# Gated linear attention in a hybrid mixer layer: level scores and state reads by 64 by 64 quarters of the matmul array

## The chip, the cores and the metric

One core of a Trainium2 chip runs the whole layer. The metric is the time of one execution on the device, in microseconds (us), and it is better when it is lower.

## What is computed

The reference is one layer over 2048 latent tokens and 256 context tokens of 1024 features. Two mixers run in parallel in both directions over the tokens: a gated linear attention (GLA, 4 heads, 64 key features, 128 value features, with a decay for each key feature), and a gated delta rule (GDN, 4 heads). Their outputs are normalised, gated and merged. The change touches GLA alone. In chunks of tokens it computes

```
diff = bi[:, :, :, None, :] - bi[:, :, None, :, :]
dec = exp(where(causal[:, :, None], diff, -inf))
att = einsum('bhtd,bhsd,bhtsd->bhts', qi, ki, dec)
o = einsum('bhtd,bhde->bhte', qi * exp(bi), s) + einsum('bhts,bhse->bhte', att, vi)
s_new = s * exp(bl)[..., None] + einsum('bhsd,bhse->bhde', ki * exp(bl - bi), vi)
```

where `bi` is the running sum of the log decay, `s` the state, and `t`, `s` are query and key tokens. The forward and the backward direction are added.

## The kernel before

The kernel has three stages. The first (up to some 1386 us) projects the input with matmuls, runs the short convolution and solves the triangular systems of GDN. The second, `phase_mix`, scans over the 16 latent chunks of 128 tokens, forward from the first and backward from the last at the same time. The third (from some 1796 us) multiplies by the output weights. Only the scan is touched.

For one chunk GLA needs the scores of 128 keys by 128 queries for 4 heads, where the decay depends on key, query and feature. It builds them by levels: at level m (64, 32, 16, 8, 4, 2) the keys of one block of m tokens meet the queries of the neighbouring block, both scaled by decays that are counted from the border between the two, so that one matmul over 64 features gives the scores of all such pairs. Forward and backward scores share a matrix, as one lies above the diagonal and the other below. The pairs of neighbours (m = 1) and the diagonal come from products of single features (`gla_ones`, `gla_near`, and `diag` from the first stage).

The parts of a step, in the order in which `gla_step` (L1263) gives them out; every `yield` is a place where `weave` (L1412) may let another generator go on, in proportion to the weights given in `phase_mix` (24 for `gla_step`, 12 for each direction of `gdn_scan`), and the framework then places the instructions on each engine's queue by its own planning:

- `gla_split` and L1268: the log decays as two fp32r parts (ACT and POOL); the diagonal into the score tile `at` (POOL).
- `gla_ends` (L1120): sums of decays by matmuls with a constant (L1117), exponentials on ACT (L1126, L1128), keys times decays on POOL (L1129).
- For the previous step: `gla_near` (L1234) finishes its scores, `gla_state` (L1306) makes the new states (L1313, L1323).
- `gla_group` (L1191), three times, for levels 64 and 32, then 16 and 8, then 4 and 2: sums (L1117), exponentials (L1205, L1208), queries times decays on DVE (L1214) and keys times decays on POOL (L1215).
- For the previous step: `gla_out` (L1327) multiplies scores by values (L1332) and scaled queries by the state (L1337) into two PSUM banks, one for the even and one for the odd heads; its `done` copies them out (ACT L1345 in the first eight steps, DVE L1347 with the earlier output added in the other eight).
- `gla_lev` (L1243), three times, one for each group: the level matmuls (L1250) into a slot of the PSUM tile `lv`, then the copies from the slot into `at`: level 64 by two copies on ACT (L1258), the others by a predicated copy on DVE with a mask from `am` (L1261). The first call is placed behind gla_out of the previous step, the second after the third group, the third at the end of the step.

The tile `lv` has two slots of 128 queries; `slot` takes them in turn. Each level matmul uses 64 rows of the array (the features of one head) and all 128 columns, so that the two heads of a pair can run at once. In the first eight steps the outputs of a chunk are written to memory; in the other eight the chunk's other direction is read back, added and normalised (`finish`, L1383: squares on ACT L1392 to L1394, scaling on POOL L1395, transposes L1399, DVE L1400).

Of the kernel before, what the change touches and what calls it, by code (L numbers as in the profile page):

```python
# [11 lines left out]
F32 = mybir.dt.float32  # L12
# [3 lines left out]
I32 = mybir.dt.int32  # L16
AF = mybir.ActivationFunctionType
ALU = mybir.AluOpType
AX = mybir.AxisListType
PSUM = bass.MemoryType.PSUM  # L20
DRAM = bass.MemoryType.DRAM

P = 128
# [7 lines left out]
NCTX = CTX // P  # L31
# [7 lines left out]
LEVELS = (64, 32, 16, 8, 4, 2, 1)  # L39
# [45 lines left out]
def const_i32():  # L85
    s = np.arange(P)[:, None]
    out = np.zeros((P, 2, len(MASK_LEVELS), 64), np.int32)
    for d in range(2):
        for i, m in enumerate(MASK_LEVELS):
            t = later_cols(d, m)[None, :]  # L90
            out[:, d, i, :] = ((s // (2 * m)) == (t // (2 * m))) & ((s // m) != (t // m))
    t = s.T
    pairs = [((s // (2 * m)) == (t // (2 * m))) & ((s // m) != (t // m)) for m in LEVELS[1:]]
    return np.concatenate([out.reshape(P, -1), *[x.astype(np.int32) for x in pairs]], 1)


class Build:
# [1045 lines left out]
    def slot(self):  # L1143
        self.nslot += 1
        return self.lv[:, :, self.nslot % 2]

# [44 lines left out]
    def gla_group(self, r, i0):  # L1191
        nc, q, k, at = self.nc, r["q"], r["k"], r["at"]
        E = self.gE.tile([P, 2, 2, 2, P], F32, name="E", bufs=3)
        ql = self.gq.tile([P, 2, 2, P], F32, name="ql", bufs=3)
        cols = (2 * P + i0 * P, 4 * P + i0 * P)
        for ct in range(2):
            ps = self.pe()
# [3 lines left out]
            for li in range(2):  # L1201
                m = LEVELS[i0 + li]
                s = ps[:, 256 * li:256 * li + 256]
# [12 lines left out]
        yield  # L1216
        return [(at, [E[:, ct, li, 1] for ct in range(2)], ql[:, li], LEVELS[i0 + li]) for li in range(2)]

# [15 lines left out]
    def gla_near(self, r):  # L1234
        nc, at, w = self.nc, r["at"], r["near"]
        pd = self.pe()
        for ct in range(2):
            nc.tensor.matmul(pd[:, 2 * ct:2 * ct + 2], w[:, ct], self.bones, start=True, stop=True)
        B = [P, 4, P]
        nc.vector.copy_predicated(at, self.am[:, len(LEVELS) - 2].unsqueeze(1).broadcast_to(B),  # L1240
                                  pd[:, 0:4].unsqueeze(2).broadcast_to(B))

    def gla_lev(self, levs, behind=None):  # L1243
        nc, got = self.nc, []
        for at, ks, ql, m in levs:
            ps = self.slot()
            for ct in range(2):
                for hp in range(2):
                    rows = slice(64 * hp, 64 * hp + 64)
                    mm = nc.tensor.matmul(ps[:, hp, ct], ks[ct][rows], ql[rows, ct], start=True, stop=True)  # L1250
                    self.behind(mm, behind)
                    self.last_lev = mm
            got.append((self.byhalf(at), ps, m))
        for at, ps, m in got:
            if m == 64:
                for x in range(2):
                    rows, cols = slice(64 * x, 64 * x + 64), slice(64 - 64 * x, 128 - 64 * x)
                    nc.scalar.copy(at[rows, :, :, cols], ps[rows, :, :, cols])  # L1258
            else:
                i = LEVELS.index(m) - 1  # L1260
                nc.vector.copy_predicated(at, self.am[:, i].unsqueeze(1).unsqueeze(1).broadcast_to([P, 2, 2, P]), ps)  # L1261

    def gla_step(self, f, b, prev):  # L1263
        nc = self.nc
        self.gla_split(f)
        self.gla_split(b)
        at = f["at"] = f["kp"].tile([P, 4, P], F32, name="at", bufs=1)
        nc.gpsimd.tensor_tensor(at, self.diag[:, f["c"] - NCTX, :].unsqueeze(2).broadcast_to([P, 4, P]),  # L1268
                                self.ident.unsqueeze(1).broadcast_to([P, 4, P]), op=ALU.mult)
        yield  # L1270
        self.gla_ends(f)
        yield
        if prev is not None:
            self.gla_near(prev[0])
            S = self.gla_state(prev)
            yield
        levs = yield from self.gla_group(f, 0)
# [6 lines left out]
        if prev is not None:  # L1284
            out, done = self.gla_out(prev, S)
        self.gla_lev(levs, out if prev is not None else None)
        if prev is not None:
# [4 lines left out]
        last = yield from self.gla_group(f, 4)  # L1292
        yield
        self.gla_lev(more)
        yield
# [31 lines left out]
    def gla_out(self, pair, S):  # L1327
        nc = self.nc
# [5 lines left out]
        for d, r in enumerate(pair):  # L1334
            for h in range(4):
                ct, rows = h // 2, slice(64 * (h % 2), 64 * (h % 2) + 64)
                mm = nc.tensor.matmul(po[h % 2][:, d, ct], r["qe"][rows, ct], S[d][rows, ct], start=False,  # L1337
                                      stop=d == 1 and h >= 2, skip_group_check=True)

# [82 lines left out]
    def phase_mix(self):  # L1422
# [14 lines left out]
        for x in range(2):  # L1437
            nc.vector.memset(self.bones[64 * x:64 * x + 64, x:x + 1], 1.0)
            nc.vector.memset(self.bones[64 * x:64 * x + 64, 1 - x:2 - x], 0.0)
        self.am = mp.tile([P, len(LEVELS) - 1, P], I32, name="am")  # L1440
        wt = mp.tile([P, 2, WL], F32R, name="wt")
# [3 lines left out]
        self.ppe = self.pool("ppe", 3, PSUM, ctx=ctx)  # L1445
        self.lv = self.pool("ppg", 1, PSUM, ctx=gctx).tile([P, 2, 2, 2, P], F32, name="lv")
        self.nslot, self.last_lev = 0, None
# [246 lines left out]
```

## Time and profile before

| | us |
|---|---|
| median of 3 runs | 2175.05 |
| lowest and highest | 2174.11 to 2176.63 |
| the profiled execution | 2176.2 |
| its span, first to last instruction | 2174.4 |
| TensorE marked busy | 2089.3 (96%) |
| DVE, ACT, POOL busy | 1237.0, 888.1, 867.7 |

The profile is one execution of its own. A busy TensorE is not one at its peak, because matmuls are pipelined and the marked time of each runs to its end; how close their starts stand tells more. The chain of work that ended last is followed back from the last instruction, at each step to what released it or to the instruction before it on its engine. An fp32 matmul stands in the records as two matmuls, each with its weight load (PEld). A row of windows gives the busy time, with the number of instructions, in the order TensorE (PE), its weight loads (PEld), DVE, ACT, POOL, those that were asked for.

### The profile page before, as it was taken

Reading aid. Unit: us, or ns where it says so; the run is one execution under the profiler, and the core shown is the slowest. Engines: PE = TensorE matmul, PEld = TensorE weight load, DVE = VectorE, ACT = ScalarE, POOL = GpSimd, SP = SyncE. Lnnn points to the kernel's source line nnn. Section 1 sums busy time; section 2 is a strip of 40 time slices with the busy share of each in tenths; the row PEclk is TensorE's granted clock in tenths of the full one; section 3 lists DMA queues with packets and bytes.
Section 4 is the critical chain, followed back from the end, with each engine's and each line's share of the span. In section 5 each row is a group of like instructions: output and inputs, shape, how many; then the busy total and the mean of one; then the engine's idle time right before and its main releaser. Section 6 shows DMA issues by size and latency. Waiting matters only on the chain.

```text
span 2174.4 us, 39781 instructions
## 1 busy us (share of the span) xinstructions
PE 2089.3 (96%) x15072; PEld 1753.6 (81%) x15072; DVE 1237.0 (57%) x2183; ACT 888.1 (41%) x2180; POOL 867.7 (40%) x779
## 2 busy tenths in 40 slices
PE   5999999999999999999999999899989988999998
PEld 2688888888888888777777777788888887999888
DVE  3813555556777554555555555566678876344333
ACT  3644255554552223343444443344455554112111
POOL 2410122222231015665666662556566655222331
PEclk9999999999999999999999999999999989999999
DMA  7323122222222224344444443878779958443322
GB/s 279 110 85 115 50 68 64 67 62 66 61 65 81 74 84 138 118 146 146 141 147 151 129 139 114 300 279 307 262 262 312 299 177 265 131 127 116 102 85 81
DMA packets 275004, 315.67 MB, mean 145 GB/s; under 512 B 22280, under 2 KB 206716, under 8 KB 274812
## 3 DMA queue, kind: packets, MB, share of 16 engines
q1 hardware_dynamic: 274812, 313.12, 44.5%
q8 instruction: 119, 1.95, 0.4%
q14 instruction: 73, 0.60, 0.1%
HBM read 203.20 MB, written 109.84 MB: 144 GB/s over the span
## 4 chain that ended last, share of the span: by engine, by line
PE 83%; DVE 5%; ACT 4%; DMA 4%; issue 2%; SPq 1%; POOL 1%; DVEq 0%; POOLq 0%; ACTq 0%
PE pz L370 46%; PE pz L1647 8%; PE pm L1578 7%; PE pe L1117 2%; PE pz L1079 1%; PE pe L935 1%; PE pl L987 1%; PE pl L994 1%; PE lv L1250 1%; PE pl L995 1%; DMA g<-dg 1%; PE pz L1058 1%; DVE ql L1214 1%; PE pq L613 1%; ACT E L1208 1%
## 5 line engine op out<-in xcount | busy, mean ns | idle before, releaser
L370 PE MATMUL pz<-hi,wh 128*128 128x512 f32 (+1 forms) x1560 | 621.7, 399 | 1.6 <-DVE hi L133 1.6
L370 PE MATMUL pz<-lo,wh 128*128 128x512 f32 (+1 forms) x1560 | 600.6, 385 | 1.8 <-POOL lo L134 1.8
L370 PE MATMUL pz<-hi,wl 128*128 128x512 f32 (+1 forms) x1520 | 588.6, 387 | 0.0
L370 PEld LDWEIGHTS pz<-lo,wh 128*128 128x128 f32 x1560 | 294.8, 189 | 51.3 <-POOL lo L134 3.7
L370 PEld LDWEIGHTS pz<-hi,wh 128*128 128x128 f32 x1560 | 294.4, 189 | 48.0 <-DVE hi L133 2.5
L370 PEld LDWEIGHTS pz<-hi,wl 128*128 128x128 f32 x1520 | 286.3, 188 | 53.8 <-issue 0.4
L134 POOL TENSOR_TENSOR wl<-w,wh 128x1024 fp32r<-128x1024 f32 x44 | 108.8, 2475 | 437.3 <-ACT wh L131 311.9
L568 DVE SCALAR_TENSOR_TENSOR acc<-zpad,cw,acc 128x1024 f32<-128x1024 f32 x192 | 271.4, 1414 | 6.7
L1578 PE MATMUL pm<-yh,wab 128*128 128x256 f32 x1024 | 190.5, 287 | 0.9 <-ACT wab L131 0.9
L872 DVE CAST_PREDICATED U<-kit,pl 128x256 f16<-128x256 int32 x216 | 91.2, 431 | 139.4 <-PE pl L995 135.6
L1578 PEld LDWEIGHTS pm<-yh,wab 128*128 128x128 f32 x1024 | 163.5, 195 | 1.8 <-ACT wab L131 1.0
L1647 PE MATMUL pz<-wo,mh 128*128 128x512 f32 (+1 forms) x528 | 160.6, 387 | 0.0
L1578 PE MATMUL pm<-yl,wab 128*128 128x256 f32 x512 | 146.9, 287 | 0.2 <-POOL yl L134 0.2
L988 ACT CAST ppb<-pl 128x256 f16<-128x256 f32 x216 | 73.6, 374 | 167.6 <-PE pl L987 161.2
L1215 POOL TENSOR_TENSOR E<-E,ak 128x256 f32<-128x256 f32 x96 | 80.9, 863 | 101.8 <-ACT E L1205 51.6
L1647 PEld LDWEIGHTS pz<-wo,mh 128*128 128x128 f32 x528 | 98.2, 189 | 20.0
L134 DVE TENSOR_TENSOR sql<-sq,sqh 128x512 fp32r<-128x512 f32 (+1 forms) x36 | 28.0, 804 | 142.0 <-ACT sqh L131 141.8
L623 POOL TENSOR_TENSOR acc<-acc,sq 128x512 f32<-128x512 f32 x32 | 51.1, 1605 | 138.4 <-ACT sq L622 90.6
L1647 PE MATMUL pz<-wo,ml 128*128 128x512 f32 (+1 forms) x264 | 101.5, 385 | 0.0
L1578 PEld LDWEIGHTS pm<-yl,wab 128*128 128x128 f32 x512 | 100.2, 196 | 0.7 <-POOL yl L134 0.4
L134 POOL TENSOR_TENSOR yl<-wr,yh 128x1024 fp32r<-128x1024 f32 x16 | 40.2, 2529 | 135.7 <-ACT yh L131 135.7
L1652 DVE TENSOR_TENSOR mt<-pz,gtb 128x512 f32<-128x512 f32 (+1 forms) x33 | 22.3, 675 | 117.0 <-PE pz L1647 114.8
(297 smaller groups left out, 4182.9 us busy)
## 6 DMA issues: line engine op xcount, KB each, us to landing
dgate<-ob SPq DMA_DIRECT2D x96, 256.0 KB
gd<-dgd SPq DMA_DIRECT2D x32, 768.0 KB
w<-in_w_in SPq DMA_DIRECT2D x44, 512.0 KB
qk<-dqkv SPq DMA_DIRECT2D x32, 512.0 KB
ga<-dgate SPq DMA_DIRECT2D x64, 256.0 KB
dqkv<-acc SPq DMA_DIRECT2D x192, 64.0 KB
dgd<-tm SPq DMA_DIRECT2D x36, 256.0 KB
dgd<-n SPq DMA_DIRECT2D x36, 256.0 KB
```

What stands on the lines that cost most here:

```text
L134: getattr(nc, lo).tensor_tensor(dst_lo, src, dst_hi.bitcast(F32), op=ALU.subtract)
L370: nc.tensor.matmul(ps[:, 0:n], a[:, kk, :], b[:, kk, :], start=(k == 0), stop=(k == last - 1))
L568: nc.vector.scalar_tensor_tensor(acc, src, wcol, acc, op0=ALU.mult, op1=ALU.add)
L613: nc.tensor.matmul(u[4][:, 0:u[2]], self.ones, u[3][i], start=(i == 0), stop=(i == 1))
L623: nc.gpsimd.tensor_tensor(v, v, r, op=ALU.mult)
L872: self.nc.vector.copy_predicated(out, mv, data)
L988: nc.scalar.copy(ppl, pc.rearrange("p h (j i) -> p h j i", i=m))
L1117: self.nc.tensor.matmul(out, g[:, i, ct * P:(ct + 1) * P], self.wt[:, d, cols[0]:cols[1]], start=(j == 0), stop=(j == 1))
L1215: nc.gpsimd.tensor_tensor(E[:, :, li, 1], E[:, :, li, 1], k, op=ALU.mult)
L1578: nc.tensor.matmul(ps[:, half * 256:half * 256 + 256], wab[wi][:, k, j * P:(j + 1) * P], yy[:, k, :], start=(i == 0), stop=(i == 11))
L1647: nc.tensor.matmul(ps, aa[:, k, i * P:(i + 1) * P], wo[k][wi][:, cs], start=(j == 0), stop=(j == 23))
L1652: nc.vector.tensor_tensor(sq, ps, gtb[:, cs], op=ALU.mult)
```

## The change

Scores within the two halves of a chunk (levels 32 and below) go into a tile `own` of 128 keys by 64 queries, where each key holds the queries of its own half; level 64 goes into the other two quarters of `at` as before. Each level matmul of 64 features, 128 keys and 128 queries becomes two of 64 features, 64 keys and 64 queries, that write the keys' half of the partitions. `lv` has four slots of 64 queries. Masks, the diagonal and the predicated copies have half the size. `gla_near` finishes `own` and then copies it on ACT into `at`. The first `gla_lev` call takes the first two groups, four levels, at once; the second call is gone. In `gla_out` the queries with the state are cut into halves of 64 queries as well.

```diff
+    own = [np.where(s < 64, x[:, 0:64], x[:, 64:128]) for x in pairs]
+    return np.concatenate([out.reshape(P, -1), *[x.astype(np.int32) for x in own]], 1)
...
-        return self.lv[:, :, self.nslot % 2]
+        return self.lv[:, :, self.nslot % 4]
...
     def gla_near(self, r):
-        nc, at, w = self.nc, r["at"], r["near"]
+        nc, at, own, w = self.nc, r["at"], r["own"], r["near"]
...
-        B = [P, 4, P]
-        nc.vector.copy_predicated(at, self.am[:, len(LEVELS) - 2].unsqueeze(1).broadcast_to(B),
+        B = [P, 4, 64]
+        nc.vector.copy_predicated(own, self.am[:, len(LEVELS) - 2].unsqueeze(1).broadcast_to(B),
                                   pd[:, 0:4].unsqueeze(2).broadcast_to(B))
+        for x in range(2):
+            half = slice(64 * x, 64 * x + 64)
+            nc.scalar.copy(at[half, :, half], own[half])
 
     def gla_lev(self, levs, behind=None):
         nc, got = self.nc, []
-        for at, ks, ql, m in levs:
+        for r, ks, ql, m in levs:
             ps = self.slot()
             for ct in range(2):
-                for hp in range(2):
-                    rows = slice(64 * hp, 64 * hp + 64)
-                    mm = nc.tensor.matmul(ps[:, hp, ct], ks[ct][rows], ql[rows, ct], start=True, stop=True)
-                    self.behind(mm, behind)
-                    self.last_lev = mm
-            got.append((self.byhalf(at), ps, m))
-        for at, ps, m in got:
+                for x in range(2):
+                    y = x if m < 64 else 1 - x
+                    keys, qs = slice(64 * x, 64 * x + 64), slice(64 * y, 64 * y + 64)
+                    for hp in range(2):
+                        rows = slice(64 * hp, 64 * hp + 64)
+                        mm = nc.tensor.matmul(ps[keys, hp, ct], ks[ct][rows, keys], ql[rows, ct, qs], start=True, stop=True)
+                        self.behind(mm, behind)
+                        self.last_lev = mm
+            got.append((r, ps, m))
+        for r, ps, m in got:
             if m == 64:
                 for x in range(2):
                     rows, cols = slice(64 * x, 64 * x + 64), slice(64 - 64 * x, 128 - 64 * x)
-                    nc.scalar.copy(at[rows, :, :, cols], ps[rows, :, :, cols])
+                    nc.scalar.copy(self.byhalf(r["at"])[rows, :, :, cols], ps[rows])
             else:
                 i = LEVELS.index(m) - 1
-                nc.vector.copy_predicated(at, self.am[:, i].unsqueeze(1).unsqueeze(1).broadcast_to([P, 2, 2, P]), ps)
+                nc.vector.copy_predicated(self.byhalf(r["own"]),
+                                          self.am[:, i].unsqueeze(1).unsqueeze(1).broadcast_to([P, 2, 2, 64]), ps)
 
     def gla_step(self, f, b, prev):
...
+        f["at"] = f["kp"].tile([P, 4, P], F32, name="at", bufs=1)
+        own = f["own"] = f["kp"].tile([P, 4, 64], F32, name="own", bufs=1)
+        nc.gpsimd.tensor_tensor(own, self.diag[:, f["c"] - NCTX, :].unsqueeze(2).broadcast_to([P, 4, 64]),
+                                self.id64.unsqueeze(1).broadcast_to([P, 4, 64]), op=ALU.mult)
...
-        self.gla_lev(levs, out if prev is not None else None)
+        self.gla_lev(levs + more, out if prev is not None else None)
         if prev is not None:
             done()
             yield
             yield from self.gla_put(prev)
         yield
         last = yield from self.gla_group(f, 4)
-        yield
-        self.gla_lev(more)
         yield
...
     (gla_out)
         for d, r in enumerate(pair):
-            for h in range(4):
-                ct, rows = h // 2, slice(64 * (h % 2), 64 * (h % 2) + 64)
-                mm = nc.tensor.matmul(po[h % 2][:, d, ct], r["qe"][rows, ct], S[d][rows, ct], start=False,
-                                      stop=d == 1 and h >= 2, skip_group_check=True)
+            for ct in range(2):
+                for x in range(2):
+                    half = slice(64 * x, 64 * x + 64)
+                    for hp in range(2):
+                        rows = slice(64 * hp, 64 * hp + 64)
+                        mm = nc.tensor.matmul(po[hp][half, d, ct], r["qe"][rows, ct, half], S[d][rows, ct], start=False,
+                                              stop=d == 1 and ct == 1, skip_group_check=True)
...
     (phase_mix)
-        self.am = mp.tile([P, len(LEVELS) - 1, P], I32, name="am")
+        self.am = mp.tile([P, len(LEVELS) - 1, 64], I32, name="am")
+        self.id64 = mp.tile([P, 64], F32, name="id64")
+        for x in range(2):
+            half = slice(64 * x, 64 * x + 64)
+            nc.vector.tensor_copy(self.id64[half], self.ident[half, half])
...
-        self.lv = self.pool("ppg", 1, PSUM, ctx=gctx).tile([P, 2, 2, 2, P], F32, name="lv")
+        self.lv = self.pool("ppg", 1, PSUM, ctx=gctx).tile([P, 2, 4, 2, 64], F32, name="lv")
```

## Rows read from the trace of the kernel before

**Rows 1.** Windows: length, busy by engine (instructions), clock granted, DMA share, GB/s.
```profile
1386.00:1600.00 214.00, 199.75 (x1965) 182.68 (x1964) 147.04 (x311) 99.58 (x383) 123.28 (x144) 0.99 0.83 287
1600.00:1796.00 196.00, 176.61 (x1639) 163.77 (x1638) 156.97 (x327) 109.91 (x514) 126.86 (x137) 0.97 0.81 262
1635.00:1713.00 78.00, 70.72 (x683) 65.26 (x682) 64.42 (x138) 45.69 (x222) 52.63 (x61) 1.00 0.96 315
```

**Rows 2.** The chain that ended last, by line: 1386 to 1600, then 1600 to 1796.
```profile
by line: PE lv L1250 9.1%; PE pz L1079 8.5%; DVE ql L1214 8.4%; ACT oi L1063 6.1%; PE pz L1047 5.9%; DMA g<-dg 5.7%; issue 5.5%; PE pe L1117 5.4%; DMA av<-dav 4.0%; PE pz L1337 3.7%; DMA do<-oi 3.7%; PE pz L1313 3.7%; PE pz L1058 3.2%; PE p
...
by line: PE pe L1117 8.8%; ACT E L1208 6.6%; DMA g<-dg 6.5%; PE pz L1089 6.4%; PE pz L1079 6.4%; issue 6.0%; PE pz L1058 5.9%; PE pe L1399 5.5%; PE pz L1337 3.8%; PE lv L1250 3.4%; DVE og L1347 3.3%; PE pz L1332 3.2%; DVE at L1261 3.1%; DMA
```

**Rows 3.** Timeline of step A, TensorE's matmuls: start, us, engine, line, operation, idle before.
```profile
1561.33 0.94 PE L1332 MATMUL pz<-av,at 128*128 128x128 f32 x6 [0.43 <-DVE oi L1090]
...
1562.19 1.16 PE L1337 MATMUL pz<-Sa,q 64*128 64x128 f32 x16
...
1563.19 1.06 PE L1250 MATMUL lv<-ql,E 64*128 64x128 f32 x16
...
1564.18 0.39 PE L1117 MATMUL pe<-wt,gh 128*128 128x256 f32 x1
...
1564.40 0.28 PE L1117 MATMUL pe<-wt,gl 128*128 128x256 f32 x1
...
1564.52 0.28 PE L1117 MATMUL pe<-wt,gh 128*128 128x256 f32 x1
...
1569.37 1.16 PE L1250 MATMUL lv<-ql,E 64*128 64x128 f32 x16
```

**Rows 4.** Groups by line: busy us, mean ns | idle before, what ended it.
```profile
L1250 PE MATMUL lv<-ql,E 64*128 64x128 f32 x768 | 55.1, 283 | 10.3 <-DVE at L1261 9.7
...
L1261 DVE COPY_PREDICATED at<-am,lv 128x512 f32<-128x512 int32 x80 | 58.3, 729 | 42.6 <-ACT at L1258 38.0 <-PE lv L1250 4.2
...
L1258 ACT COPY at<-lv 64x256 f32<-64x256 f32 x32 | 11.7, 365 | 2.2 <-PE lv L1250 2.1
...
L872 DVE CAST_PREDICATED U<-kit,pl 128x256 f16<-128x256 int32 x216 | 91.2, 431 | 139.4 <-PE pl L995 135.6 <-PE pl L978 3.6
```

**Rows 5.** Windows of L645 alone; TensorE's timeline, first and last of 16.
```profile
1447.90:1447.93 0.03, 0.02 (x4) 0.02 (x4) 1.00 0.76 146
...
1447.90:1449.35 1.45, 1.44 (x24) 0.68 (x24) 1.00 0.95 268
...
1043.86 0.19 PE L994 MATMUL pl<-ppb,Tm 128*128 128x64 f16 x1
...
1044.29 0.19 PE L995 MATMUL pl<-Tm,ppb 128*128 128x64 f16 x1
```

**Rows 6.** Timeline of step A, POOL and ACT.
```profile
1560.35 1.59 POOL L1215 TENSOR_TENSOR E<-E,ak 128x256 f32<-128x256 f32 x2
...
1566.32 1.67 POOL L1215 TENSOR_TENSOR E<-E,ak 128x256 f32<-128x256 f32 x2 [2.94 <-ACT E L1208]
...
1569.47 0.73 POOL L1231 TENSOR_TENSOR qk<-qk,ak 128x256 f32<-128x256 f32 x1 [1.49 <-DVE qk L1230]
...
1573.15 0.62 ACT L131 CAST gh<-g 128x512 fp32r<-128x512 f32 x1 [3.49 <-DMA g<-dg]
...
1574.30 0.19 ACT L1128 COPY dec<-E 128x2 f32<-128x2 f32 x1
```

**Rows 7.** Timeline of step B, all engines.
```profile
1747.00 0.55 PE L1238 MATMUL pe<-bones,qk 128*128 128x2 f32 x4
...
1749.04 0.18 ACT L1128 COPY dec<-E 128x2 f32<-128x2 f32 x1
...
1751.06 0.72 DVE L1240 COPY_PREDICATED at<-am,pe 128x512 f32<-128x512 int32 x1
...
1751.71 1.04 POOL L1395 TENSOR_TENSOR og<-og,fss 128x512 f32<-128x512 f32 x1 [0.45 <-ACT fss L1394]
...
1753.42 0.60 PE L1399 MATMUL pe<-kf,og 128*128 128x128 f32 x4
```

More of the change, by code (lines that the diff above doesn't have):

```diff
@@ L93, in const_i32 @@
     pairs = [((s // (2 * m)) == (t // (2 * m))) & ((s // m) != (t // m)) for m in LEVELS[1:]]
-    return np.concatenate([out.reshape(P, -1), *[x.astype(np.int32) for x in pairs]], 1)
+    own = [np.where(s < 64, x[:, 0:64], x[:, 64:128]) for x in pairs]
+    return np.concatenate([out.reshape(P, -1), *[x.astype(np.int32) for x in own]], 1)
 class Build:
@@ L1191, in gla_group @@
     def gla_group(self, r, i0):
-        nc, q, k, at = self.nc, r["q"], r["k"], r["at"]
+        nc, q, k = self.nc, r["q"], r["k"]
         E = self.gE.tile([P, 2, 2, 2, P], F32, name="E", bufs=3)
@@ L1216, in gla_group @@
         yield
-        return [(at, [E[:, ct, li, 1] for ct in range(2)], ql[:, li], LEVELS[i0 + li]) for li in range(2)]
+        return [(r, [E[:, ct, li, 1] for ct in range(2)], ql[:, li], LEVELS[i0 + li]) for li in range(2)]
     def gla_ones(self, r):
@@ L1266, in gla_step @@
         self.gla_split(b)
-        at = f["at"] = f["kp"].tile([P, 4, P], F32, name="at", bufs=1)
-        nc.gpsimd.tensor_tensor(at, self.diag[:, f["c"] - NCTX, :].unsqueeze(2).broadcast_to([P, 4, P]),
-                                self.ident.unsqueeze(1).broadcast_to([P, 4, P]), op=ALU.mult)
+        f["at"] = f["kp"].tile([P, 4, P], F32, name="at", bufs=1)
+        own = f["own"] = f["kp"].tile([P, 4, 64], F32, name="own", bufs=1)
+        nc.gpsimd.tensor_tensor(own, self.diag[:, f["c"] - NCTX, :].unsqueeze(2).broadcast_to([P, 4, 64]),
+                                self.id64.unsqueeze(1).broadcast_to([P, 4, 64]), op=ALU.mult)
         yield
```

## The prediction

> **What bounds the kernel now.** I read first the windows of busy time, then the chain that ended last, by line, then one step of the sequence in the timeline of each engine. The changed code runs only in the scan, 1386 to 1796 us. There [rows 1] no single resource is at its limit: TensorE is marked busy for 199.75 of 214 us and 176.61 of 196, but that counts the modelled tails of matmuls; the DMA share is 0.83 and 0.81, with 0.96 in the three steps of 1635 to 1713. The chain [rows 2] goes from engine to engine: in the first half the level matmuls (L1250) hold 9.1%, 19.5 us, in the second half 3.4%, 6.7 us, beside DVE's level copies (L1261), 3.1%. So 26 us of the chain are matmuls that the change touches, and what they may give back is what the next waiter leaves.
>
> The sixteen steps are of two kinds. The first eight write each output for the first time, the other eight read it back and finish it. I take one of each, 1561 to 1585 (A) and 1738 to 1763 (B).
>
> **TensorE: the level matmuls.** An fp32 matmul stands as two records, so a level is 8 records now and 16 after, a burst of two levels 16 and 32. In A [rows 3] gla_out's 16 records take 1.00 us from their start to the levels' start. A record is 0.28 us long in the mean [rows 4], so the seven rounds of two ahead of the last take 1.06 - 0.28 = 0.78, 0.111 us each. Eight rounds are 0.89. A change of the array's shape costs 0.19 us on the way in (six records of L1332 would take 0.67 at that pace, the next form starts after 0.86) and 0.20 on the way out (0.10 until L1117 starts, and its second matmul comes 0.22 after the first where the third follows in 0.12). A step has one burst behind gla_out (0.89) and two alone (0.89 + 0.4 each): 3.47 us.
>
> After, a record has 64 columns in place of 128, and four quadrants can run at once. If they do, a round of four takes half of 0.111, 0.055. The four levels behind gla_out are 64 records, 16 rounds, 0.89; the last two levels are 8 rounds and two changes of shape, 0.84. That is 1.73, so 1.7 us a step less. gla_out itself becomes 32 records in quadrants with 128 columns: 8 rounds of 0.111, 0.89 as before, nothing gained; it only gets the shape that the levels behind it have.
>
> No row shows quadrants of 64 by 64, so I bound the pace. The slow end is the fastest stream that one can see for long: 16 matmuls of 64 columns in f16 start 29 ns apart (1043.86 to 1044.29) [rows 5]. At 29 ns the records cost 1.86 + 0.93 + 0.4 = 3.19, a gain of 0.28 only. The fast end is the 0.055 round, 14 ns a record. Beside it stand the column strips of L645: four matmuls with their four weight loads start within 28 ns [rows 5], and 24 take 1.45 us, the work of four strips at once. I take the fast end, because these fp32 records in strips are nearest in kind, and keep the slow one as a rival.
>
> By the Trainium skill (TensorE: Matmul & The Clock Gate, Part 1) starts of matmuls never come closer than about 25 ns, however few their columns; by that the 96 records of a step would take 2.4 us and the two changes of shape 0.4, estimated 2.8 in all, a gain of 0.7. Part 3 of the page gives about 4 ns between tiles that run together. The four starts within 28 ns speak for the second; for a long stream no run here shows either.
>
> **DVE, ACT, POOL.** Five level copies of 729 ns [rows 4] and the near copy of the same size go from 512 to 256 elements; L872, a predicated copy of 256 elements, takes 431. So each loses 0.30 us, 1.8 a step on DVE. The wait of the first copy for ACT's cross-half copies goes as well (38.0 us in all [rows 4]), because the two now write different tiles; and with four slots TensorE no longer waits for DVE before the second burst (9.7 us). ACT's cross-half copies keep their 256 elements (365 ns). gla_near adds two ACT copies of 64 x 256: bounded by 0.19 (the 128 x 2 copy, L1128 [rows 6]) and 0.37 each, I take 0.37, as the elements are the same, 0.75 a step. The diagonal product on POOL halves; nothing wants it before gla_near in the next step, so it counts nothing. The masks' load halves and two small id64 copies run once, in front of the scan's first steps, beside its loads: nothing, and 0.9 us at most (twice the 0.43 of L872).
>
> **Step A.** The chain runs through gla_out, ACT's og, at and E, one DVE copy, the middle burst, the next scan's matmuls and the last burst. After, the copy and the middle burst are out of it. The next to be late is POOL's second L1215, done at 1567.99 [rows 6], which the last burst reads: it can start 1.4 us earlier than at 1569.37 [rows 3] and is 0.45 shorter. The near product (L1231) ends at 1570.20 and stands ahead of gla_state; its inputs move up by about the middle burst's 1.1 us, so I give 0.5 back: gla_state and L1058 come 1.3 earlier. Behind L1058 the chain goes through ACT (the eight L1063), and the two new copies stand there: minus 0.75 if they are queued ahead of L1063, nothing if behind. Net 0.55 to 1.3; I take 0.9. The four levels at once need the second group's keys from POOL before gla_out ends; in A that product is done at 1561.94 (the two of 1560.35, 1.59 us [rows 6]), 1.2 us ahead of 1563.19, so no wait is added. Eight steps: 7 us.
>
> **Step B.** The last burst stands behind L1238 (1747.00 [rows 7]) and waits 0.2 us more for the DVE copy that frees its slots. L1238 hangs on DVE's queue, which loses one 0.43 copy ahead of it, so some 0.3 comes from there, 0.2 from the slots and 0.45 from the shorter burst: 0.9 us. But the finished outputs come last from POOL at 1752.75 (L1395), and their transposes ran at 1753.42, 0.6 us behind. So 0.6 is the most, and ACT, which makes their sums, has 0.75 more to do. I take 0.3 for the five steps outside 1635 to 1713, nothing in the three that DMA fills: 1.5 us. At the end of the scan three copies and the near copy hold the next stage's buffers: 4 x 0.3 plus 0.45 for the last burst, less 0.75 for the ACT copies, gives 0.9.
>
> **Sum.** 7 + 1.5 + 0.9 is 9.4, and I say 10 us, as DVE's 1.8 a step must open a queue somewhere. The profiled execution took 2176.2 (span 2174.4 and 1.8 around it), so 2166; it lies 1.15 above the median of 2175.05, so 2165.0. About 0.2%, 4.4 us, is what a measurement of this kernel can tell from no change.
>
> **Rivals.**
> (1) The stream doesn't flow: quadrants run two by two, or records come no faster than 29 ns. Then the change does not do what it says on TensorE. The four levels take 1.86, L1117 starts 0.97 later, ACT's E and POOL follow by some 0.7, the last burst is 0.5 longer than forecast, and of A's 1.3 us about 0.1 is left against up to 0.75 of ACT copies. 2175, from 2171 to 2178. Against it: the four starts in 28 ns. Chance 0.20.
> (2) The load of g takes the place of the burst. In A ACT stood idle for it 3.49 us, until 1573.15, and went from its cast without a gap to L1126 and L1128 [rows 6]: all behind that follows its landing. Its buffer is freed by the transposes L1226, which move up by the middle burst's 1.1 us and let the load be issued earlier, but the DMA share is 0.83. If it doesn't land earlier, A gains nothing and pays up to 0.75, 3 us in eight steps at half of that, which B's and the end's 2.4 repay: 2175. Chance 0.16.
> (3) Slower: the near copies stand in ACT's queue behind L1128 and wait for DVE's near copy. In B L1128 ended at 1749.22 and L1240 at 1751.78 [rows 7]; squares of the finished outputs stand behind on ACT. The price is 2.56 + 0.75 = 3.3 us, 8 times 26; with DVE 1.5 us earlier it is 1.8, 14. Against A's 7: 2182 to 2194. It decides from a hold of 0.2 us on, as 0.75 + 0.2 times 8 eats A's gain. Against it: nothing forces that place in the queue. Chance 0.12.
> (4) More: both halves pass on what TensorE and DVE save without a new wait: 8 x 1.3 in A, 8 x 0.6 in B and 0.9 at the end are 16 us, 2159 at the median; all 26 us of the chain's level matmuls would give 2149. I put 2155. Chance 0.06.
>
> **How the numbers follow.** The forecast has 0.46, with 2158 to 2170. Faster by over 0.2%: 0.46 + 0.06 + 0.06 of (1) + 0.02 of (2) = 0.60. Within 0.2%: 0.12 of (1) + 0.14 of (2) = 0.26. Slower: 0.02 of (1) and (3) = 0.14. The range 2156 to 2179 leaves out half of (4) and most of (3).
>
> **What would show it.** In the profile after: 64 level records behind gla_out in about 0.9 us (1.8 under (1)), a gap of no more than 0.1 us between the two forms; predicated copies near 430 ns, no longer idle for ACT; the last burst released by POOL's or DVE's products, not by a copy; the wait of ACT for g (2) or for the near copy (3). I am wrong if the burst takes 0.9 and the steps of kind A still last 23 us.

## The result and the profile after

The kernel after takes 2162.19 us (2158.29 to 2168.17) beside 2175.84 (2172.71 to 2177.08) of the kernel before on the same chip: ratio 0.9942, 95% interval 0.9925 to 0.9958. Measured a second time, it takes 2166.95 (2163.13 to 2168.91) beside 2175.63: 0.9954, 0.9940 to 0.9969. By the ratios that is 10 to 13 us faster (by the medians 8.7 and 13.7), where 10 were forecast. But the gain does not lie where the forecast put it.

First the parts that the change touches. Groups by line of the kernel after, 1380 to 1782 us: busy us, mean ns | idle before, what ended it. They answer to [rows 4].

```profile
L1268 DVE COPY_PREDICATED own<-am,lv 128x256 f32<-128x256 int32 x80 | 35.3, 441 | 41.5 <-ACT at L1265 40.6 <-PE lv L1257 0.5
L1257 PE MATMUL lv<-ql,E 64*64 64x64 f32 x1536 | 31.4, 221 | 10.6 <-DVE own L1268 6.7 <-POOL E L1216 3.8
...
L1245 ACT COPY at<-own 64x256 f32<-64x256 f32 x32 | 12.8, 399 | 3.3 <-DVE own L1241 2.9
L1265 ACT COPY at<-lv 64x256 f32<-64x256 f32 x32 | 11.7, 364 | 3.4 <-PE lv L1257 3.2
```

Timeline of a step of kind A in the kernel after, TensorE, DVE and ACT. It answers to [rows 3].

```profile
1549.10 0.94 PE L1339 MATMUL pz<-av,at 128*128 128x128 f32 x6 [0.25 <-DVE oi L1091]
1549.96 1.10 PE L1347 MATMUL pz<-Sa,q 64*64 64x128 f32 x32
1550.88 1.11 PE L1257 MATMUL lv<-ql,E 64*64 64x64 f32 x64
1551.93 0.39 PE L1118 MATMUL pe<-wt,gh 128*128 128x256 f32 x1
...
1554.95 0.46 PE L1257 MATMUL lv<-ql,E 64*64 64x64 f32 x16
1555.78 0.46 PE L1257 MATMUL lv<-ql,E 64*64 64x64 f32 x16 [0.36 <-POOL E L1216]
...
1552.86 0.93 DVE L1268 COPY_PREDICATED own<-am,lv 128x256 f32<-128x256 int32 x2 [3.22 <-ACT at L1265]
...
1562.22 0.62 ACT L132 CAST gh<-g 128x512 fp32r<-128x512 f32 x1 [3.48 <-DMA g<-dg]
1562.74 0.81 ACT L1245 COPY at<-own 64x256 f32<-64x256 f32 x2
1563.58 2.17 ACT L1064 ACTIVATE oi<-pz,eg 128x128 f32<-128x128 f32 x8
```

Four levels, 64 records, follow gla_out without a gap and are done in 1.05 us. The middle burst is gone. The last burst of this step is released by POOL's product, as forecast; from the ninth step on a copy of DVE still releases it six times (the 6.7 us of L1257). What did not go is DVE's wait for ACT, 40.6 us, where 38.0 stood in [rows 4], and ACT's wait for g in this step, 3.48 us, where 3.49 stood in [rows 6].

To see where the time went I cut the scan at the starts of the output matmuls (L1332 before, L1339 after): A is the eight steps from the first to the ninth, B the six from the ninth to the fifteenth, and the end is all from there on. Each kernel has two profiles; here are the windows of the second ones, the kernel before and then the kernel after (columns as in [rows 1]).

```profile
1412.00:1605.50 193.50, 178.42 (x1764) 162.43 (x1763) 130.90 (x269) 90.31 (x348) 113.24 (x133) 1.00 0.82 282
1605.50:1761.80 156.30, 142.71 (x1375) 131.81 (x1374) 128.83 (x277) 91.22 (x445) 103.06 (x117) 1.00 0.89 285
1761.80:2173.10 411.30, 389.76 (x2534) 355.29 (x2533) 189.65 (x298) 97.16 (x251) 131.50 (x114) 0.98 0.40 129
```

```profile
1412.60:1594.80 182.20, 167.47 (x2274) 153.59 (x2273) 119.83 (x269) 96.75 (x362) 108.66 (x131) 0.99 0.84 289
1594.80:1760.00 165.20, 143.73 (x1760) 133.69 (x1760) 121.34 (x277) 95.14 (x459) 101.27 (x116) 0.93 0.88 283
1760.00:2165.20 405.20, 384.52 (x2614) 350.61 (x2612) 188.68 (x298) 97.64 (x253) 129.67 (x114) 0.98 0.40 131
```

A lost 11.3 us, the end 6.1, and **B became 8.9 us longer**. In the first profiles the three are 191.8, 155.8 and 411.0 before, and 184.1, 159.8 and 404.3 after. The means: A 9.5 us shorter, B 6.4 longer, the end 6.4 shorter, and the first step comes 2.0 earlier, in code that is nearly all the same and where the two profiles of before differ by 3.8. Together that is 11.5, as the four spans have it (2173.75 to 2162.25, means of two).

The eight steps of A did not gain alike. The fifth alone went from 26.0 and 25.8 us to 22.2 and 22.1, which is 3.7 of the 9.5. The seventh, on which the prediction worked A out, went from 23.3 and 23.7 to 23.6 and 24.6 (the last at a clock of 0.93). Here are the two in the first profile of the kernel before, with a wait in the fifth, and then in the first of the kernel after.

```profile
1511.90:1537.91 26.01, 23.43 (x214) 21.72 (x213) 15.56 (x33) 11.20 (x44) 13.80 (x17) 0.93 0.84 276
1560.51:1583.80 23.29, 21.56 (x214) 20.06 (x213) 15.57 (x33) 12.38 (x45) 13.78 (x17) 1.00 0.74 244
...
ACT gh L131 <- DMA g<-dg: 7.5, 1, 7.5
```

```profile
1503.71:1525.95 22.24, 20.05 (x279) 18.77 (x277) 14.87 (x33) 12.27 (x47) 13.97 (x18) 1.00 0.86 304
1548.46:1572.09 23.63, 20.56 (x278) 18.90 (x277) 13.88 (x32) 13.18 (x47) 13.29 (x17) 1.00 0.77 270
```

In the fifth step of the kernel before ACT stands idle for g for 7.5 us (7.3 in the second profile); in the kernel after it has no such wait there. Ahead of that load, in the queue of SyncE that issues the loads, the kernel before has four loads of gates (L1388), issued in the fourth step, and two of the next stage's weights (L1531), with two more right behind it; in the kernel after the framework's plan has all eight in the sixth to eighth. No run parts the place of these loads from the pace of the matmuls, so the cause of this part of the gain stays open.

The whole set, from one profile each, with the stages cut at the unrounded starts. "Last burst" and "merge" are counted from the fifteenth step's output matmuls: the start of the scan's last level matmuls, and the start of the next stage's first cast (`yh`). "Clock" is the mean granted clock in B.

```
kernel                      ratio  (interval)       A      B      clock  last burst  merge  end
before, first profile                               191.9  155.7  1.00   13.7        19.2   411.1
before, again               0.9996 (0.9984-1.0008)  193.5  156.4  1.00   13.0        17.6   411.2
after, first profile        0.9942 (0.9925-0.9958)  184.0  159.8  0.97    7.6        12.6   404.3
after, again                0.9954 (0.9940-0.9969)  182.3  165.2  0.93    7.6        12.6   405.2
quarters alone              0.9968 (0.9958-0.9977)  183.7  161.4  0.98   11.9        15.3   412.4
three bursts                0.9969 (0.9957-0.9980)  184.8  162.8  0.94   10.3        15.2   408.8
state by rows               0.9967 (0.9955-0.9978)  184.3  161.6  0.94    7.6        12.7   409.0
DVE refilled                0.9996 (0.9985-1.0007)  186.9  165.6  0.93   10.9        16.6   408.1
near copies on POOL         0.9954 (0.9940-0.9967)  183.2  163.9  0.96    7.6        11.5   405.3
g in three buffers          0.9957 (0.9943-0.9972)  182.8  164.4  0.93    7.6        12.6   404.8
DVE's copies first          0.9960 (0.9944-0.9975)  185.2  156.0  0.98    7.2        12.2   405.2
after, no gate loads        0.9934 (0.9922-0.9947)  181.2  159.4  0.96    7.9        12.9   406.0
before, no gate loads       0.9993 (0.9984-1.0002)  191.1  157.6  1.00   13.0        17.6   408.1
before, finish behind merge 0.9999 (0.9990-1.0008)  195.4  159.0  0.98   12.8        17.5   410.6
```

The framework plans each queue's order anew for every edit, so a ratio holds the edit and what the plan made of it. A profiled execution need not lie at its kernel's median: those of quarters alone, three bursts, state by rows, and finish behind the merge lie 3.5 to 4.1 us above it, that of DVE's copies first 6.9 below, the others within 1.5. The second run of the kernel after was expected at 2160 to 2165 us with 183 to 186 in A, and came out just outside both; the second of before was expected at 188 to 193 in A, 154 to 159 in B and 410 to 412 at the end, and only A came out just outside. The ratios were taken on several occasions, each beside runs of the kernel before. Stages of one kernel repeat within about 2 us in A and 1 us at the end, but by 5 in B.

### The profile page after: what moved, and what is told of

Its sections match the earlier page's. It is cut to its first block, busy times and chain, and to the rows that moved or that the text cites. A ratio compares the mean times of both kernels' runs of the same rounds, so it can differ in the third digit from the quotient of the medians.

```text
span 2159.3 us, 41811 instructions
## 1 busy us (share of the span) xinstructions
PE 2062.3 (96%) x16096; PEld 1730.3 (80%) x16096; DVE 1215.5 (56%) x2185; ACT 899.0 (42%) x2212; POOL 858.6 (40%) x779
## 4 chain that ended last, share of the span: by engine, by line
PE 82%; DVE 5%; ACT 5%; DMA 3%; POOL 2%; issue 2%; SPq 1%; DVEq 0%; POOLq 0%; ACTq 0%
PE pz L371 46%; PE pz L1661 8%; PE pm L1592 8%; DMA g<-dg 2%; PE pe L936 1%; PE pe L1118 1%; PE pl L995 1%; PE pl L988 1%; PE pl L996 1%; PE pz L1080 1%; DVE ql L1215 1%; ACT E L1209 1%; PE pz L1059 1%; PE pq L614 1%; PE pz L1347 1%
```

## The experiments

**One part of the change alone: the quarters.**

```diff
...
-                    mm = nc.tensor.matmul(ps[:, hp, ct], ks[ct][rows], ql[rows, ct], start=True, stop=True)
...
+                        mm = nc.tensor.matmul(ps[keys, hp, ct, qs], ks[ct][rows, keys], ql[rows, ct, qs], start=True, stop=True)
...
```

> The kernel before, with one part of the change alone: the level matmuls go by quarters of 64 features, 64 keys and 64 queries, in the two slots of 128 queries as before; copies, masks, gla_out and the three bursts of two levels stay (the slots' unwritten quarters are zeroed once). Theory (TensorE's bursts are most of the gain): three bursts a step lose 0.45 us each, the first and the middle or last one of them on the chain, some 0.9 us in eight steps of kind A: 2167 to 2170. Rival (the gain is DVE's, by the halved copies, or the merging of two bursts): 2174 to 2178, as before.

2168.71 us beside 2175.46: 7 us faster. A takes 183.7 us, as in the kernel after. So A's gain does not need the halved copies or the merged bursts, as far as one profile can show. But the matmuls' pace is not shown to make all of it: the plan moved the loads of gates and weights here as well, and the fifth step is down to 22.2 us. B is longer here too (161.4), with the old copies and three bursts, so that loss comes with the quarters. At the end the next stage starts 15.3 us behind the fifteenth step, which is half of the gain, and here it is lost again further on (412.4).

**Without the merging of two bursts.**

```diff
-        self.gla_lev(levs + more, out if prev is not None else None)
+        self.gla_lev(levs, out if prev is not None else None)
...
+        self.gla_lev(more)
+        yield
```

> The kernel after, with the middle burst of two levels back at its own place behind the third group of levels; quarters, half copies, four slots and gla_out as after. Theory (the middle burst's way off the chain is a part of the gain): its 0.45 us, two changes of shape of 0.2 and the copies behind it come back in eight steps of kind A, some 0.6 each: 2166 to 2169. Rival (with short bursts its place is indifferent, as POOL's E times k is late anyway): 2160 to 2164, as after.

2167.95 us. The interval overlaps with that of the kernel after's second measurement, so the time doesn't decide. A is 0.8 to 2.6 us longer, which is no more than profiles of one kernel differ by. What stands out is that the last burst starts 2.7 us later (10.3 against 7.6) and the next stage 2.6.

**gla_out's state matmuls by rows, as before.**

```diff
...
-                        mm = nc.tensor.matmul(po[hp][half, d, ct], r["qe"][rows, ct, half], S[d][rows, ct], start=False,
...
+                mm = nc.tensor.matmul(po[h % 2][:, d, ct], r["qe"][rows, ct], S[d][rows, ct], start=False,
...
```

> The kernel after, with gla_out's state matmuls as before, whole 128 queries by two rows of the array (16 records instead of 32), levels as after. The prediction gave this part nothing but the shape: gla_out 0.89 us either way, and one more change of shape of 0.2 us ahead of the levels. Theory: 0.2 us in eight to sixteen steps, 2162 to 2165. Rival (the state matmuls by quarters cost more than they save, as twice the records have to be started): faster than after, 2158 to 2161.

2167.31 us. It is not faster than after, so the rival falls. The price that the theory names is too small to be told: A takes 184.3 us, within what one kernel's profiles differ by.

**DVE's old time given back.**

```diff
+                nc.vector.copy_predicated(self.byhalf(r["own"])[:, :, 0],
+                                          self.am[:, i].unsqueeze(1).broadcast_to([P, 2, 64]), ps[:, :, 0])
...
+        nc.vector.copy_predicated(own[:, 0:2], self.am[:, len(LEVELS) - 2].unsqueeze(1).broadcast_to([P, 2, 64]),
+                                  pd[:, 0:2].unsqueeze(2).broadcast_to([P, 2, 64]))
```

> The kernel after, with DVE's old time given back: behind each of the six predicated copies of a step (five levels and the near one, 441 ns) the same copy is done again for half of the heads, 128 elements, an estimated 0.30 us by the 729 ns of 512 and the 441 of 256 elements. Nothing of the result changes. Theory (the shorter copies are on the way): DVE's 1.8 us a step costs 0.3 to 0.6 us in each of sixteen steps, 2167 to 2172. Rival (DVE waits for ACT's cross-half copies and for ql's E anyway, so its work is covered): 2160 to 2164, as after.

2175.02 us beside 2175.46: the whole gain is gone, more than the theory asked for. A second copy took 292 ns, so 1.75 us a step. The last burst starts 3.3 us later and the next stage 4.0, so DVE is on the way at the end. A is 3.7 us longer than after, but 3.0 of them stand in the third step alone (24.9 against 21.9), where the granted clock is 0.93; the other seven are 0.7 longer together, so a price in every step of A is not shown. The plan's order changes with this edit too, and one profile can't part the two.

**The near copies on POOL.**

```diff
-            nc.scalar.copy(at[half, :, half], own[half])
+            nc.gpsimd.tensor_copy(at[half, :, half], own[half])
```

> The kernel after, with the two new copies of the near part (64 x 256, 0.40 us each on ACT) on POOL. The order of the other work stays nearly as it is. Theory (ACT pays for them, as the prediction has it: they stand ahead of the eight scaled outputs of GDN in A): 0.4 to 0.8 us less in eight steps, 3 to 6 us faster than after, 2156 to 2160. Rival (POOL needs more than ACT for a copy, and its keys times decays, which the last burst awaits, come later): 2162 to 2168.

2165.67 us beside 2166.95 for after beside it: no difference. A is 183.2 us against 182.3. A copy takes 394 ns on POOL and 399 on ACT. The theory falls. The time lies in the rival's range, but not for its reason, as POOL takes no longer. What the two copies cost at all is not shown, as no run leaves them out; on ACT they cost no more than on POOL.

**Three buffers for g.**

```diff
-            r["g"] = wk.tile([P, 2 - d, 256], F32, name=f"g{d}")[:, 0:n]
+            r["g"] = wk.tile([P, 2 - d, 256], F32, name=f"g{d}", bufs=3)[:, 0:n]
```

> The kernel after, with three buffers for the log decays g instead of two, so that their load can be issued a step earlier; otherwise nothing is changed. Theory (the second rival of the prediction: the steps of kind B gained nothing, because ACT waits for the landing of g, 30.9 us in the scan, 20 us of it on the chain of the second half): 4 to 10 us faster than after, 2152 to 2158, and ACT's wait for g under 10 us. Rival (the DMA engines are 0.82 to 0.93 busy there, so that another load is late in its place): 2160 to 2164.

2168.15 us, the same as after. Waits within B, one line each: the kernel before again, the kernel after, and this one.

```profile
ACT gh L131 <- DMA g<-dg: 3.5, 4, 1.9
```

```profile
ACT gh L132 <- DMA g<-dg: 11.3, 5, 4.8
```

```profile
ACT gh L132 <- DMA g<-dg: 1.4, 2, 1.0
```

The wait of ACT for g did grow in B, from 3.5 to 11.3 us. A third buffer takes most of it away there (in A it stays, 16.7 us), and B stays at 164.4 us. So g's landing is not what makes B long.

**DVE's copies ahead of ACT's.**

```diff
-        for r, ps, m in got:
+        for r, ps, m in sorted(got, key=lambda x: x[2] == 64):
```

> The kernel after, with the order of the copies within one call of the level function turned: the predicated copies on DVE first, then ACT's two copies of level 64. The prediction held that DVE no longer waits for ACT, as the two write different tiles; it still waits 40.6 us. Theory (what ties them is the tile lv that both read, whose slots share two banks, and the framework lets one engine into them after the other, in the order of the code): DVE's wait for ACT falls under 5 us, ACT waits for DVE instead, about 16 times 1.4 us, and E's exponentials are placed ahead of it; time 2158 to 2166. Rival (DVE's wait is for something else that ACT does first, such as its exponentials): the wait stays near 40 us.

Waits from 1380 to 1790 us, the kernel after again and then this one.

```profile
DVE own L1268 <- ACT at L1265: 40.7, 16, 3.2
...
PE lv L1257 <- DVE own L1268: 6.8, 6, 1.5
```

```profile
DVE own L1268 <- PE lv L1257: 21.5, 16, 2.7
```

DVE no longer waits for ACT, only for the matmuls. So its wait was for its turn at the tile `lv`, which both engines read, in the order of the code. ACT did not wait for DVE, as I had thought it would: the plan put exponentials ahead of its copies. The time, 2166.96 us, is that of after (2166.95), with an interval of the ratio from 0.9944 to 0.9975. So the 40 us were covered, to within some 3 us. B takes 156.0 us in this profile, but that execution was the fastest of its kernel, 6.9 us below the median.

**Without the gate loads, after and before.**

```diff
-        nc.sync.dma_start(y, self.d_gate[l // 2, :, 4 * mi:4 * mi + 4, (l % 2) * P:(l % 2) * P + P])
...
-        nc.vector.scalar_tensor_tensor(self.flat(y), pt, self.pc[:, 64 + mi:65 + mi], self.flat(y),
-                                       op0=ALU.mult, op1=ALU.mult)
+        nc.vector.scalar_tensor_tensor(y, self.heads(pt), self.pc[:, 64 + mi:65 + mi],
+                                       self.ident.unsqueeze(1).broadcast_to([P, 4, P]), op0=ALU.mult, op1=ALU.mult)
```

> The kernel after without the load of the gates in the finish (32 loads of 256 KB, some 8 MB that fall into the steps of kind B and the end); the product takes the identity matrix in their place, so that the outputs are not gated in that product. Beside the next kernel, the same of before, it asks whether the transfers set the pace of B. Theory (they do: that is why nothing of the change arrives there): six steps of B take 150 us or less instead of 160 to 165, and the distance between the two kernels without the loads grows to 15 us or more. Rival (B is a chain of engines and g's landing stands in it, whatever the share): B within 3 us of after, and the distance as with the loads, 8 to 13.

> The kernel before without the same gate loads, with the identity in their place. Theory (transfers set the pace of B): B falls from 156 to 150, and the kernel gains less than after does by the same cut, 5 to 10 us: 2166 to 2171. Rival (a chain of engines): B as before and 2172 to 2176.

2159.37 and 2172.42 us, 13.1 apart. The windows of B, the kernel after and then the kernel before, both without the loads:

```profile
1591.80:1751.10 159.30, 138.94 (x1760) 129.36 (x1759) 120.87 (x276) 94.75 (x458) 102.32 (x117) 0.96 0.79 250
```

```profile
1603.40:1761.00 157.60, 142.53 (x1375) 131.81 (x1374) 128.83 (x277) 91.22 (x445) 102.98 (x117) 1.00 0.76 245
```

The DMA share falls from 0.88 and 0.89 to 0.76 in the kernel before, and its B stays (157.6 against 155.8 and 156.3). Transfers don't set B's pace there. In the kernel after, B is as long as in its first profile (159.8) and shorter than in its second. No B comes to 150 us and the distance is the rival's, so the theory that transfers hold back the change's gain in B falls. In A of the kernel before, where four of the gates' loads are gone from the fourth step, the fifth step lasts 24.0 us, and 5.5 of the wait for g are left.

**The finish behind the merge, in the kernel before.**

```diff
-                self.fin_rest(4)
+                self.fin_rest(4, self.last_pm)
...
+                                self.behind(mm, None if bi else self.last_pm)
```

> The kernel before, with nothing of the change: only the last four finishers' transposes, and the first output matmuls, are ordered behind the last merge matmul of the first block, where the framework places them in the kernel after by itself. In the profile before, TensorE waits 3.9 us for POOL's scaling ahead of the first of these transposes, with the merge's matmuls behind it. Theory (some of the change's gain behind the scan, 411 to 405 us, is that place in TensorE's queue): from the last step on 406 to 408 us, time 2171 to 2173. Rival (the end starts when weights and scores are there, whatever the place): 410 to 412 and 2174 to 2177.

2174.08 us, as before, and the end takes 410.6 us. The place of those transposes in TensorE's queue is not the reason for the end's gain.

None of the variants of the kernel after is faster than it, with its whole computation.

## What B gives back

What is left to explain is that B's steps are longer after. By the windows above TensorE is not marked busy for 13.6 us of B before and for 21.5 after (156.30 less 142.71, 165.20 less 143.73): what the quarters save there became idle time. The granted clock in B was 1.00 in both profiles of before and 0.97 and 0.93 after. The second profile of the kernel after in slices of 2 us, around the middle of a step of B:

```profile
1654.00:1656.00 2.00, 1.69 (x16) 1.50 (x14) 0.75 (x3) 1.93 (x11) 0.23 (x1) 1.00 0.97 333
1656.00:1658.00 2.00, 1.12 (x34) 0.89 (x34) 2.00 (x6) 1.94 (x13) 2.00 (x3) 1.00 0.97 350
1658.00:1660.00 2.00, 0.99 (x12) 0.78 (x5) 2.00 (x7) 1.97 (x10) 1.77 (x3) 0.79 0.82 312
1660.00:1662.00 2.00, 2.00 (x17) 1.98 (x19) 1.75 (x7) 1.16 (x6) 2.00 (x4) 0.50 0.74 219
1662.00:1664.00 2.00, 2.00 (x13) 1.67 (x10) 1.12 (x4) 1.92 (x10) 2.00 (x2) 0.50 0.46 134
1664.00:1666.00 2.00, 2.00 (x12) 2.00 (x11) 0.66 (x1) 1.15 (x6) 1.36 (x3) 0.50 0.44 116
```

And TensorE's timeline there:

```profile
1656.09 0.39 PE L1118 MATMUL pe<-wt,gh 128*128 128x256 f32 x1 [0.40 <-ACT E L1209]
...
1657.38 0.70 PE L1257 MATMUL lv<-ql,E 64*64 64x64 f32 x32 [0.79 <-DVE own L1268]
...
1659.52 1.01 PE L1239 MATMUL pe<-bones,qk 128*128 128x2 f32 x4 [1.01 <-POOL qk L1232]
```

TensorE waits for ACT, then for DVE and then for POOL; the short burst no longer fills the time between. Behind these waits the granted clock is 0.50, which is 1.2 GHz instead of 2.4, from 1659 to 1666, and the work that stands there takes longer. In this profile four of B's six steps hold such a stretch; they last 28.2, 27.5, 28.6 and 28.0 us. The two without last 26.8 and 26.1, and the six of the kernel before 27.1, 27.1, 26.0, 25.6, 25.4 and 25.1, all at full clock. The means are 28.1 and 26.45, so four such stretches are some 6.5 of the 8.9 us. In the first profile of after two steps hold one (27.3 and 26.4), and the longest, 28.8, holds none: there TensorE stands 2.88 us idle ahead of the finish's transposes. So the clock is the larger part in one profile and a smaller one in the other. Over the whole table B takes 155.7 to 157.6 us where the clock is 1.00, 156.0 to 163.9 at 0.96 to 0.98, and 161.6 to 165.6 at 0.93 and 0.94; the kernel before too takes 159.0 us in the one profile where its clock falls (0.98, the last row). No run kept TensorE busy there to hold the clock up; that it causes the loss is read from the rows, and not shown by an edit.

## Why the end became shorter

Timelines of the second profiles, TensorE, DVE and ACT: the kernel before, where the fifteenth step begins at 1761.8, and the kernel after, where it begins at 1760.0. The last line of the first is a slice as above.

```profile
1771.04 2.48 PE L1047 MATMUL pz<-Sb,qk 128*128 128x128 f32 x10
1773.31 1.60 PE L1058 MATMUL pz<-Sb,qk 128*128 128x128 f32 x8
1774.84 1.16 PE L1250 MATMUL lv<-ql,E 64*128 64x128 f32 x16
...
1778.62 0.72 DVE L1240 COPY_PREDICATED at<-am,pe 128x512 f32<-128x512 int32 x1
...
1779.42 1.99 ACT L131 CAST yh<-wr 128x1024 fp32r<-128x1024 f32 x2 [4.51 <-DVE at L1240]
...
1772.00:1774.00 2.00, 2.00 (x12) 2.00 (x11) 2.00 (x7) 1.89 (x11) 1.97 (x3) 0.50 0.00 0
```

```profile
1763.96 1.95 PE L1048 MATMUL pz<-Sb,qk 128*128 128x128 f32 x16
...
1767.60 0.69 PE L1257 MATMUL lv<-ql,E 64*64 64x64 f32 x32 [1.47 <-DVE own L1268]
...
1771.01 0.44 DVE L1241 COPY_PREDICATED own<-am,pe 128x256 f32<-128x256 int32 x1
...
1772.64 1.03 ACT L132 CAST yh<-wr 128x1024 fp32r<-128x1024 f32 x1
```

Before, the last burst comes behind a second, separate burst and behind matmuls of the delta rule (L1047, L1058). Its copies and the near copy follow, and ACT stands 4.51 us and waits for the near copy before it can begin the next stage. After, both last levels go in one burst at +7.6 us, ahead of most of L1059, the near copy is done at +11.4, and ACT works through without that wait. From that first cast on, the four profiles of before and after take the same 391.7 to 393.6 us. In the table the start of the merge moves with the last burst: three bursts give back 2.6 us of the 5.0 to 6.6, and DVE's old time 4.0.

The clock has a part here as well. In both profiles of the kernel before it falls in the fifteenth step, behind waits of TensorE for DVE and POOL (1.2 and 1.6 us) and ahead of the last burst: ten records of L1047 take 2.48 us there, where sixteen take 1.95 after at the full clock. For 3.4 us in the second profile and 4.9 in the first the clock ahead of the last burst is 0.50, and in neither profile of after. An estimate from these times is that up to 1.7 and 2.5 of the 5.4 and 6.1 us by which the last burst starts earlier are the clock's.

## Why the prediction was right, and where it was not

The time was right, and so was the likeliest case, but the sum came out by luck. B was forecast 7.9 us too good, the end 5.5 and A 2.5 too poor, and 2.0 us more came ahead of the first step, where nothing was forecast. The prediction's own sign of being wrong is half there: the burst takes 0.89 us, and the step of kind A on which it was worked out still lasts 23.6 and 24.6; the mean of the eight falls from 24.1 to 22.9.

**TensorE's pace: right.** Forecast were 0.055 us for a round of four and 0.89 for the 64 records; the row gives 1.11 less a last one of 0.22, which is 0.89 from the first start to the last, and 1.05 with the change of shape. That is 14 ns a record. By the Trainium skill (TensorE: Matmul & The Clock Gate, Part 1) starts never come closer than some 25 ns, by which those records would take an estimated 1.6 us; the trace does not agree, for quarters that run together. gla_out came to 0.92, forecast 0.89.

**DVE, ACT, POOL.** The copies: 441 ns, forecast 431. The near copies: 0.40, forecast 0.37. The step "the wait of the first copy for ACT's cross-half copies goes as well ... because the two now write different tiles" is wrong: both read one tile, `lv`, and the order in which they read it follows the code. The wait stayed, and so did 6.7 of the 9.7 us of TensorE's wait for slots that I had let go. The first wait was covered: with the copies turned it is gone, and the time is the same. The second was not tried by itself.

**Step A: near in size, not in place.** 7 us were forecast (0.9 a step); 9.5 were measured. The step that I worked out, the seventh, gained nothing. ACT waits for g there as before, 3.5 us (3.7 in the second profile), and the two near copies stand ahead of L1064, as feared; that is rival (2), in the place where I put it. What A gained is 3.7 us in the fifth step, which the prediction never looked at, with its wait for g, and 0.5 to 1.5 in each of the other six. Moving the near copies to POOL made no difference, so the 0.75 that I took off for them on ACT is not seen.

**Step B: wrong.** Forecast was a gain of 1.5 us in eight steps; measured is a loss of 6.4 in six, the last two being part of my end. "I take 0.3 for the five steps outside 1635 to 1713, nothing in the three that DMA fills" counts the time that TensorE saves as a gain or as nothing. It became idle time, and behind it the granted clock fell. ACT's wait for g grew in B as well, from 2.8 and 3.5 us to 11.3 and 13.9 (in A it fell, from 24.0 and 26.2 to 18.5 and 16.7); the third buffer shows that it is not the bound of B.

**The end: mis-sized.** Forecast 0.9, measured 6.4. I added up the shorter instructions and left out that one burst fewer moves the last one ahead of the delta rule's matmuls, with the wait of ACT for the near copy behind it, and that the clock falls there in the kernel before.

**The rivals.** The stream flows, so (1) is out. (2) holds in the step on which it was read, but not over A as a whole. (3), ACT held by the near copies, did not come: L1245 waits 2.9 us for DVE in the whole scan, and the copies on POOL gave the same time. (4) was not reached. DVE's shorter copies may have been priced low: the forecast lets them carry a part of the 2.4 us of B and the end, and one copy of A's chain, while giving DVE its old time back took 8 us (2175.02 less 2166.95), with a plan of its own.

## What to carry to other kernels

Where an engine's work is cut in a stage that others pace, ask what it does with the time that it gains: TensorE's may become idle time and then a lower clock, and the stage gets longer than it was. At the border to a next stage, look for the one late instruction that the next stage waits for, and follow what stands ahead of it in its queue; moving it was worth more here (6.4 us) than the durations said (0.9). And cut the trace of both kernels into the same stages and steps, twice, before a sum that agrees is taken for an explanation: here one step of eight held 3.7 of 9.5 us, and not the step that was worked out.

## What was not expected of the hardware

Quarters of 64 by 64 in fp32, forecast but in no row before, take 14 ns a record over 64 records, where two row halves with 128 columns took 0.111 us for two, worked out from [rows 3]. A copy of 64 x 256 in fp32 from SBUF to SBUF takes as long on POOL (394 ns) as on ACT (399). TensorE's granted clock fell behind short waits in the middle of a step, and stayed at 1.2 GHz for some 3 to 7 us, more often in the kernel that gives TensorE less to do (two and four such stretches in B of its two profiles, and none before).
